# A decoder layer in float32: sums of squares on another engine, later forms, and form tiles at other offsets

## The chip, the cores and the metric

The kernel runs on one core of a Trainium2 chip, in one launch. The metric is the device time of that core in microseconds. Five engines run their own instruction streams: TensorE (matmuls), VectorE (DVE), ScalarE (ACT), GpSimd (POOL) and SyncE, which here issues DMAs. An engine takes its instructions in the order in which the program lists them, and one that waits holds all that stand behind it.

## The reference

One layer of a hybrid decoder: 512 tokens, width 2048, all float32. What matters here is its second half.

```python
mix = jnp.concatenate([ya, yb, yc], axis=-1)                 # three kinds of attention, normed
x = x + jnp.einsum('bse,ed->bsd', mix, w_out)
h = rmsnorm(x, ffn_norm)                                     # x / sqrt(mean(x*x)) * gain
u = causal_dwconv(jnp.einsum('bsd,df->bsf', h, w_up), conv_w, conv_b)    # width 3 along the tokens
gate, up = jnp.split(u, [D_FF], axis=-1)                     # D_FF = 5632
x = x + jnp.einsum('bsf,fd->bsd', jax.nn.silu(gate) * up, w_down)
```

## The kernel before

Activations lie with features on the partitions and the 512 tokens along the free axis, in 16 blocks of 128 features ("x block m", m = 0..15). Every float32 matrix is split into a high part, a cast to the matmul's format, and a low part, the rest. A product is three matmuls: high x high, low x high, high x low. Casts run on ACT, rests on DVE.

**Order.** The program is one long list that Python generators write: each task issues a few instructions and yields, and a clock in the kernel (lines 22 to 113) books every instruction on a model of its engine (for DVE 0.2 us + elements per partition/960, for GpSimd 0.2 + /480) and lets a task go on when the model says that its engine is there. What an engine executes is the order in which tasks came to write. Since every compute operation is recorded through one helper, all have line 51 in the profile; SyncE's DMAs have line 129, GpSimd's accumulating DMAs line 1044.

**Second half of the output projection.** Sixteen products (m = 0..15) of 24 matmuls of 128x512 accumulate into `pj`. After each runs the task `projected(m)`: DVE multiplies `pj` by a row scale into `tq` and adds the reloaded x block (`xn`), ACT writes it scaled by the norm's gain into `xb`, SyncE stores it (`xm_dram`) and reloads block m+3 (`reload_x`, a ring of 4 buffers named `xn`), and `sumsq` squares the block on ACT and adds the square to `gacc`, on GpSimd. A buffer of `xn` can be reloaded when its old block has been stored and squared.

**Forms.** The up-projection works on pairs of x blocks (j = 0..7) and on halves of 256 tokens, with seven products in place of eight: each pair gives seven "forms" of 256 columns, the halves and sums of them, written by `even_forms(j)` (forms 0 and 3, from block 2j) and `odd_forms(j)` (forms 5, 1, 2, 4, 6). High parts are in the tiles `th0` to `th7`, low parts in `tl0` to `tl7`, 7 x 256 columns each. Sums are made in tiles `sm`. In the program before all of these tiles start 128 bytes after a multiple of 512, and the weights' `hi` and `lo` tiles on a multiple of 512.

**Up-projection.** There are 44 units of 128 rows of w_up. Each has seven steps, with the weights a11, p, q, a12, v, r, a22 and the forms 0, 3, 5, 1, 4, 2, 6 in this order; p = block(1,0) + block(1,1), v = block(0,0) + block(1,0), q = p + a11, r is made of others on DVE. A step is 8 pairs x 3 matmuls of 128x256 into `s`: for k = 0..7 high weight x `th`k, high weight x `tl`k, low weight x `th`k. In the profile they are `s<-th,hi`, `s<-tl,hi`, `s<-th,lo`; in the steps 0 and 1 of unit 0 the weights lie in `wh` and `wl`, two halves of 512 columns. a11, a12 and a22 are loaded by one DMA of 512 KB; p and v by a DMA and an accumulating one that GpSimd issues when the first has landed (`fetch`). The raw weights lie in `ld` and `wr`, three buffers each in turn. For unit 0 q is one DVE add of 128x1024 (`first_sum`, `add_raw`), made during the output projection.

Step s of the up-projection waits, in the order of writing, until `ready` has "even" or "odd" of the pair k, and step 2 until the odd forms of pair 7. The norm's factor is needed from step 6.

Of the kernel before, what the change touches and what calls it, by code (L numbers as in the profile page):

```python
# [29 lines left out]
PAD = 152  # L30
# [88 lines left out]
def program(tc, xT, w_in, w_out, w_up, w_down, small, table, consts, onehot, lognum, out):  # L119
# [24 lines left out]
    with ExitStack() as ctx:  # L144
# [175 lines left out]

        def sumsq(pool, acc, t, first):
            if first:
                scalar.activation(acc, t, AF.Square)
                return
            sq = yield from take(pool, rows[0])
            scalar.activation(sq, t, AF.Square)
            yield
            gpsimd.tensor_add(acc, acc, sq)
            give(sq)
# [613 lines left out]
        tr = tctx.enter_context(tc.tile_pool(name="tr", bufs=1, side="right", reuse_waits="tile"))  # L943
        cv = tx.tile([128, SM_N - SM_CONV], F32, name="conv")
        TH = [tp.tile([128, 7 * HS], F32R, name=f"th{j}") for j in range(8)]
        TL = [tp.tile([128, 7 * HS], F32R, name=f"tl{j}") for j in range(8)]
        load(cv, small[:, SM_CONV:])
        xs2, xb, quarters = [], [], {}

# [9 lines left out]
        def even_forms(j):  # L959

            a = xb[2 * j]
            while j > 1 and ("odd", j - 2) not in ready:
                yield 0.1
            f = quarters[j] = tr.tile([128, 4 * HS], F32, name="sm", bufs=2)
            scalar.copy(TH[j][:, :HS], a[:, :HS])
            vector.tensor_sub(f[:, :HS], a[:, :HS], a[:, HS:])
            yield
            scalar.copy(TH[j][:, 3 * HS:4 * HS], f[:, :HS])
            low(j, a[:, :HS], 0, 1)
            yield  # L970
            low(j, f[:, :HS], 3, 4)
            ready["even", j] = True

        def odd_forms(j):
            while j not in quarters:
                yield 0.1
            a, b, f = xb[2 * j], xb[2 * j + 1], quarters[j]
            q = [f[:, i * HS:(i + 1) * HS] for i in range(4)]
            vector.scalar_tensor_tensor(q[2], b[:, HS:], -1.0, q[0], op0=ALU.mult, op1=ALU.subtract)
            yield  # L980
            scalar.copy(TH[j][:, 5 * HS:6 * HS], q[2])
            scalar.copy(TH[j][:, HS:3 * HS], b)
            vector.tensor_sub(q[1], b[:, HS:], a[:, HS:])
            vector.scalar_tensor_tensor(q[3], q[2], -1.0, b[:, :HS], op0=ALU.mult, op1=ALU.subtract)
            low(j, q[2], 5, 6)
            yield
            scalar.copy(TH[j][:, 4 * HS:5 * HS], q[1])
            scalar.copy(TH[j][:, 6 * HS:], q[3])
            low(j, b, 1, 3)
            yield  # L990
            low(j, q[1], 4, 5)
            low(j, q[3], 6, 7)
            ready["odd", j] = True

        def projected(m):
            def task(pt):
                t = xs2[m]
                sq = yield from take(tx, "tq")
# [4 lines left out]
                yield  # L1003
                while m > 2 and ("odd", (m - 3) // 2) not in ready:
                    yield 0.1
# [8 lines left out]
                yield from (odd_forms if m % 2 else even_forms)(m // 2)  # L1014
                yield from sumsq(tx, acc, t, m == 0)
                if m == KT - 1:
                    yield
                    yield from row_rstd(tx, acc, D, r2, nr2)
                    ready["r2"] = True
# [14 lines left out]
        def fetch(u, name):  # L1034
# [3 lines left out]
            if u == NFF:  # L1038
                return load(t, w_down[0][DOWN.index(name)])
            first, second = {"a11": ((0, 0), None), "a12": ((0, 1), None), "a22": ((1, 1), None),  # L1040
                             "p": ((1, 0), (1, 1)), "v": ((0, 0), (1, 0))}[name]
            arrival = load(t, w_up[u, first[0], first[1]])
            if second:
                nc.gpsimd.dma_start(t, w_up[u, second[0], second[1]], accum_op=ALU.add)
                arrival += 4
            return arrival

        def add_raw(u, name, a, b):
            if u < NFF:
                first = u == 0 and name == "q"  # L1050
                t = got[u, name] = place() if first else tr.tile([128, 1024], F32, name="sm", bufs=2)
                vector.tensor_add(t, got[u, a], got[u, b])
# [22 lines left out]
        def first_sum():  # L1075
            while len(raws) < len(stream):
                yield 0.1
            yield max(raws[len(stream) - 1][1] - clock.now(), 0.01)
            fetch(0, "a12")
            add_raw(0, "q", "p", "a11")  # L1080

# [6 lines left out]
        wq = ctx.enter_context(tc.tile_pool(name="wq", bufs=1, reuse_waits="tile"))  # L1088
        while (0, "q") not in got:
            idle()  # L1090
# [16 lines left out]
        def w(t, i):  # L1107
            return cv[:, 4 * t + i:4 * t + i + 1]

# [73 lines left out]
        for s in range(7 * NFF):  # L1183
# [6 lines left out]
            if j == 3 and u + 1 < NFF:  # L1190
                for name in ("v", "a22") if u else ("a12", "v", "a22"):
                    fetch(u + 1, name)
            while s == 2 and ("odd", 7) not in ready or s == 6 and "r2" not in ready:
                idle()
# [10 lines left out]
            for k in range(8):  # L1205
                while ("even" if form in (0, 3) else "odd", k) not in ready:
                    idle()
# [156 lines left out]
```

## Time and profile before

| | us |
|---|---|
| median of 3 runs (lowest, highest) | 2162.34 (2160.52, 2177.22) |
| profiled execution | 2163.5 |
| its span | 2161.7 |
| TensorE busy in it | 2142.2 (99%) |
| DVE busy | 1460.8 (68%) |
| ACT busy | 1151.2 (53%) |
| GpSimd busy | 180.3 (8%) |

The span runs from the first to the last instruction of the profile; the time of the execution has some 2 us around it. By the chain of waits in time order attention and the input projection take the first 660 us, the output projection's second half ends at 788, the up-projection runs to about 1690 and the down-projection to the end. In a timeline row the columns are start, length, engine, line, operation, written tile <- read tiles and shape, and in brackets how long the engine was idle before and who released it. "Granted clock" 1.00 is 2.4 GHz, 0.50 is 1.2 GHz.

### The profile page before, as it was taken

To read this page: it belongs to the slowest core of one execution; us is meant where nothing else is said; L and a number is where in the kernel's file an instruction comes from. 1 tells how busy PE (TensorE), PEld (TensorE's weight loads), DVE (VectorE), ACT (ScalarE), POOL (GpSimd) and SP (SyncE) were. 2 spreads that over 40 slices of the span, in tenths; PEclk is the share of its full clock that TensorE was granted. 3 is DMA by queue.
4 is the path that set the end of the run, shared out by engine and by line. 5 is a ranking of instruction groups with operands and counts; after the bars stand their busy time and mean duration, and the time that the engine had idled before them with its cause. 6 is when DMAs were issued, how large, how long until landed. Compare 5 with 4: busy or idle time off the path is not lost.

```text
span 2161.7 us, 34584 instructions
## 1 busy us (share of the span) xinstructions
PE 2142.2 (99%) x13236; PEld 1926.7 (89%) x13236; DVE 1460.8 (68%) x2252; ACT 1151.2 (53%) x2043; POOL 180.3 (8%) x241
## 2 busy tenths in 40 slices
PE   8999999999999989999999999999999999999999
PEld 6888888888888879999999999999999888888887
DVE  7677777767765788888888888888888543322222
ACT  6778677767764555555555555555555333222221
POOL 4000101010000121000000000000000000000000
PEclk9999999999999999999999999999999999999999
DMA  6322344334566667777777777777776543533332
GB/s 198 106 93 84 100 145 137 112 102 144 194 200 200 200 178 214 186 210 194 200 198 197 209 191 198 198 200 197 198 205 179 178 166 132 173 110 117 117 117 73
DMA packets 124013, 353.82 MB, mean 164 GB/s; under 512 B 14328, under 2 KB 17784, under 8 KB 123848
## 3 DMA queue, kind: packets, MB, share of 16 engines
q1 hardware_dynamic: 111176, 305.47, 42.1%
q0 software_dynamic: 12672, 46.14, 12.9%
q8 instruction: 104, 1.70, 0.3%
q14 instruction: 61, 0.50, 0.1%
HBM read 312.18 MB, written 32.57 MB: 159 GB/s over the span
## 4 chain that ended last, share of the span: by engine, by line
PE 97%; DMA 1%; DVE 1%; issue 0%; SPq 0%; ACT 0%; POOLq 0%; DVEq 0%; ACTq 0%
PE s L51 51%; PE pj L51 42%; PE po L51 3%; PE c L51 2%; DMA wr<-in_w_up_dram 1%; SPq L129 0%; DVE wl L51 0%; DMA st<-in_xT_dram 0%; DVE sm L51 0%; DMA cst<-in_consts_dram 0%; DMA wr<-in_w_in_dram 0%; ACT x L51 0%; DVE sq L51 0%; DVE lo L51 0%; ACT hi L51 0%
## 5 line engine op out<-in xcount | busy, mean ns | idle before, releaser
L51 PE MATMUL s<-th,hi 128*128 128x256 f32 x2448 | 690.2, 282 | 1.4 <-ACT th L51 1.0
L51 PE MATMUL s<-tl,hi 128*128 128x256 f32 x2448 | 689.6, 282 | 1.3 <-DVE tl L51 1.3
L51 PE MATMUL s<-th,lo 128*128 128x256 f32 x2448 | 689.5, 282 | 0.0
L51 DVE TENSOR_TENSOR wl<-wr,wh 128x512 fp32r<-128x512 f32 (+2 forms) x424 | 297.7, 707 | 328.2 <-ACT wh L51 326.0
L51 ACT CAST wh<-wr 128x512 fp32r<-128x512 f32 (+2 forms) x424 | 252.9, 599 | 460.4 <-PE pj L51 319.7
L51 PE MATMUL pj<-x,wh 128*128 128x512 f32 x1504 | 473.5, 396 | 0.0
L51 PEld LDWEIGHTS s<-th,hi 128*128 128x128 f32 x2448 | 461.6, 189 | 2.1 <-ACT th L51 1.2
L51 PEld LDWEIGHTS s<-tl,hi 128*128 128x128 f32 x2448 | 461.5, 189 | 1.7 <-DVE tl L51 1.5
L51 PEld LDWEIGHTS s<-th,lo 128*128 128x128 f32 x2448 | 461.5, 189 | 0.0
L51 PEld LDWEIGHTS pj<-x,wh 128*128 128x128 f32 x1504 | 271.4, 188 | 51.1 <-issue 3.0
L51 PE MATMUL pj<-x,wl 128*128 128x512 f32 x752 | 294.3, 391 | 0.0
L51 PE MATMUL pj<-g,wh 128*128 128x512 f32 x620 | 190.8, 389 | 0.0
L51 DVE TENSOR_TENSOR lo<-sm,hi 128x1024 fp32r<-128x1024 f32 x87 | 106.6, 1225 | 100.5 <-ACT hi L51 100.5
L51 PEld LDWEIGHTS pj<-x,wl 128*128 128x128 f32 x752 | 141.2, 188 | 31.1
L51 ACT CAST hi<-sm 128x1024 fp32r<-128x1024 f32 x87 | 91.2, 1049 | 139.7 <-DVE sm L51 139.7
L51 DVE TENSOR_TENSOR lo<-wr,hi 128x1024 fp32r<-128x1024 f32 x111 | 135.5, 1221 | 25.9 <-ACT hi L51 25.9
L51 DVE TENSOR_TENSOR lo<-ld,hi 128x1024 fp32r<-128x1024 f32 x111 | 135.7, 1222 | 24.3 <-ACT hi L51 24.3
L51 PEld LDWEIGHTS pj<-g,wh 128*128 128x128 f32 x620 | 116.4, 188 | 24.1
L51 ACT CAST hi<-wr 128x1024 fp32r<-128x1024 f32 x111 | 116.7, 1051 | 19.7 <-PE s L51 14.7
L51 ACT CAST hi<-ld 128x1024 fp32r<-128x1024 f32 x111 | 116.6, 1050 | 18.8 <-PE s L51 15.6
L51 PE MATMUL pj<-g,wl 128*128 128x512 f32 x310 | 120.6, 389 | 0.0
L51 DVE CUSTOM_DVE_ANT_0 sc<-s,strip 128x128 f32<-128x128 f32 (+3 forms) x96 | 43.6, 455 | 74.6 <-PE s L51 74.2
(289 smaller groups left out, 3004.5 us busy)
## 6 DMA issues: line engine op xcount, KB each, us to landing
ld<-in_w_up_dram SPq DMA_DIRECT2D x111, 512.0 KB, 4.9
wr<-in_w_up_dram SPq DMA_DIRECT2D x109, 512.0 KB, 4.7
wr<-in_w_in_dram SPq DMA_DIRECT2D x78, 512.0 KB, 3.5
wr<-in_w_down_dram SPq DMA_DIRECT2D x78, 512.0 KB, 3.5
ld<-in_w_up_dram POOLq DMA_DIRECT2D x44, 512.0 KB, 5.5
wr<-in_w_up_dram POOLq DMA_DIRECT2D x44, 512.0 KB, 5.6
wr<-in_w_out_dram SPq DMA_DIRECT2D x32, 512.0 KB, 4.0
g_dram<-wl SPq DMA_DIRECT2D x44, 256.0 KB, 3.2
```

Source lines behind the costliest of these rows:

```text
L51: res = issue(out, *args, **kwargs)
```

## The change

1. `sumsq` in `projected` adds the squares to `gacc` on DVE.
2. Forms have a ready flag each. Pair 7 stops after forms 5 and 1, pair 6 before the low parts of forms 4 and 6, until step 1 of the up-projection is being written ("late"). `xb` of block m waits for form 2 of the pair that it takes the buffer from. The norm's factor is written when all sixteen squares are.
3. Unit 0's q is no DVE add but a load of block (1,0) and two accumulating DMAs, of (1,1) and of (0,0); a12 is fetched ahead of it.
4. The convolution's constants come in two loads, 152 columns into the tile `pad` (which held nothing before), 200 into `conv`. The tiles `th0` to `th6` are 16 bytes longer (their pitch becomes 7200 bytes), and a tile of 32 bytes, `end`, follows the forms. By the addresses of the program the tiles `th`j now start at 32(j-1) bytes against a multiple of 512, from -32 to 192, and all `tl`j at 192; `hi` and `lo` stay.

```diff
-        def sumsq(pool, acc, t, first):
+        def sumsq(pool, acc, t, first, engine=gpsimd):
...
-            gpsimd.tensor_add(acc, acc, sq)
+            engine.tensor_add(acc, acc, sq)
...
-        cv = tx.tile([128, SM_N - SM_CONV], F32, name="conv")
-        TH = [tp.tile([128, 7 * HS], F32R, name=f"th{j}") for j in range(8)]
+        cv = tx.tile([128, SM_N - SM_CONV - PAD], F32, name="conv")
+        TH = [tp.tile([128, 7 * HS + (4 if j < 7 else 0)], F32R, name=f"th{j}") for j in range(8)]
         TL = [tp.tile([128, 7 * HS], F32R, name=f"tl{j}") for j in range(8)]
-        load(cv, small[:, SM_CONV:])
+        vector.memset(tp.tile([128, 8], F32, name="end"), 0.0)
+        load(pad, small[:, SM_CONV:SM_CONV + PAD])
+        load(cv, small[:, SM_CONV + PAD:])
...
             scalar.copy(TH[j][:, 5 * HS:6 * HS], q[2])
             scalar.copy(TH[j][:, HS:3 * HS], b)
+            low(j, q[2], 5, 6)
+            yield
+            low(j, b[:, :HS], 1, 2)
+            ready["form 5", j] = ready["form 1", j] = True
+            while j == 7 and "late" not in ready:
+                yield 0.1
             vector.tensor_sub(q[1], b[:, HS:], a[:, HS:])
             vector.scalar_tensor_tensor(q[3], q[2], -1.0, b[:, :HS], op0=ALU.mult, op1=ALU.subtract)
-            low(j, q[2], 5, 6)
             yield
             scalar.copy(TH[j][:, 4 * HS:5 * HS], q[1])
-            scalar.copy(TH[j][:, 6 * HS:], q[3])
-            low(j, b, 1, 3)
+            scalar.copy(TH[j][:, 6 * HS:7 * HS], q[3])
+            low(j, b[:, HS:], 2, 3)
+            ready["form 2", j] = True
+            while j == 6 and "late" not in ready:
+                yield 0.1
             yield
             low(j, q[1], 4, 5)
             low(j, q[3], 6, 7)
-            ready["odd", j] = True
+            ready["form 4", j] = ready["form 6", j] = ready["odd", j] = True
 
         def projected(m):
             def task(pt):
+                while len(xs2) <= m:
+                    yield 0.1
...
-                while m > 2 and ("odd", (m - 3) // 2) not in ready:
+                while m > 2 and ("form 2", (m - 3) // 2) not in ready:
                     yield 0.1
...
-                yield from sumsq(tx, acc, t, m == 0)
-                if m == KT - 1:
+                yield from sumsq(tx, acc, t, m == 0, vector)
+                squares.append(m)
+                if len(squares) == KT:
...
-                             "p": ((1, 0), (1, 1)), "v": ((0, 0), (1, 0))}[name]
+                             "p": ((1, 0), (1, 1)), "v": ((0, 0), (1, 0)), "q": ((1, 0), (1, 1))}[name]
...
+            if name == "q":
+                nc.gpsimd.dma_start(t, w_up[u, 0, 0], accum_op=ALU.add)
+                arrival += 4
...
         def first_sum():
...
-            yield max(raws[len(stream) - 1][1] - clock.now(), 0.01)
             fetch(0, "a12")
-            add_raw(0, "q", "p", "a11")
+            yield max(fetch(0, "q") - clock.now(), 0.01)
+            ready["q"] = True
...
-            while s == 2 and ("odd", 7) not in ready or s == 6 and "r2" not in ready:
+            if s == 1:
+                ready["late"] = True
+            while s == 2 and any(("odd", x) not in ready for x in range(8)) or s == 6 and "r2" not in ready:
                 idle()
...
-                while ("even" if form in (0, 3) else "odd", k) not in ready:
+                while (f"form {form}", k) not in ready:
```

The written order moves with it, at the transition from the output projection to the up-projection. First SyncE's queue there. Before, the reloads of the x blocks 13, 14 and 15 are `xn_8031`, `xn_8090` and `xn_8141`, and the `ld` are a11, p and a12:

```order
L129 DMA xn_8031<-xab_dram_76 128x512
L129 DMA ld_8063<-in_w_up_dram 128x1024
L129 DMA xm_dram_77<-xn_7919 128x512
L129 DMA xn_8090<-xab_dram_76 128x512
L129 DMA ld_8117<-in_w_up_dram 128x1024
L129 DMA xm_dram_77<-xn_7974 128x512
L129 DMA xn_8141<-xab_dram_76 128x512
L129 DMA xm_dram_77<-xn_8031 128x512
L129 DMA ld_8201<-in_w_up_dram 128x1024
```

In the changed program the reloads of blocks 13, 14 and 15 are `xn_8046`, `xn_8191` and `xn_8196`; the three `ld` are a11, p and a12, `wr_8110` is the first block of q, `wr_8246` that of v:

```order
L129 DMA xn_8046<-xab_dram_76 128x512
L129 DMA ld_8052<-in_w_up_dram 128x1024
L129 DMA ld_8102<-in_w_up_dram 128x1024
L129 DMA ld_8108<-in_w_up_dram 128x1024
L129 DMA wr_8110<-in_w_up_dram 128x1024
L129 DMA xm_dram_77<-xn_7917 128x512
L129 DMA xn_8191<-xab_dram_76 128x512
L129 DMA xm_dram_77<-xn_8041 128x512
L129 DMA xn_8196<-xab_dram_76 128x512
L129 DMA wr_8246<-in_w_up_dram 128x1024
```

The reload of block 14 moved from between a11 and p to behind q, and that of block 15 with it.

ACT's rows of the changed program from the last split of w_out (`wh_8140`) on; `xn_7890`, `xn_7815` and `xn_8041` are the x blocks 10, 9 and 12, `wh_8212` and `wh_8268` the two halves of p:

```order
L51 CAST wh_8140<-wr_7998 128x512
L51 ACTIVATE tq1_8157<-xn_7890 128x512
L51 CAST wh_8162<-ld_8052 128x512
L51 CAST wh_8179<-ld_8052 128x512
L51 CAST th4_7408<-sm_7930 128x256 x2
L51 ACTIVATE xb_8188<-xn_7917,sm_80 128x512
L51 ACTIVATE xb_8193<-xn_8041,sm_80 128x512
L51 CAST wh_8212<-ld_8102 128x512
L51 ACTIVATE tq2_8218<-xn_7815 128x512
...
L51 CAST hi_8258<-ld_8108 128x1024
L51 CAST hi_8265<-wr_8110 128x1024
L51 CAST wh_8268<-ld_8102 128x512
L51 ACTIVATE tq1_8292<-xn_8041 128x512
```

The squares of blocks 9 and 12 now stand behind the splits of p, and that of block 12 behind those of a12 and q as well. In the program before the squares of blocks 11 (`xn_7919`) and 12 (`xn_7974`) stood between the splits of a11's two halves:

```order
L51 CAST wh_8181<-ld_8063 128x512
L51 ACTIVATE tq2_8192<-xn_7919 128x512
L51 ACTIVATE xb_8195<-xn_8031,sm_80 128x512
L51 ACTIVATE tq0_8206<-xn_7974 128x512
L51 CAST wh_8215<-ld_8063 128x512
L51 CAST wh_8233<-ld_8117 128x512
```

DVE's rows of the changed program, from the add into x block 14 (`xn_8191`) to the low form 0 of pair 6 (`tl6`); `wl_8180` is the low part of a11's second half, `tq1_8157` and `tq2_8218` are squares, `xn_8196` is block 15:

```order
L51 TENSOR_TENSOR xn_8191<-tq0_8198,xn_8191 128x512
L51 TENSOR_TENSOR wl_8180<-ld_8052,wh_8179 128x512
L51 TENSOR_TENSOR gacc_86<-gacc_86,tq1_8157 128x512
L51 SCALAR_TENSOR_TENSOR sm_8079<-xb_8188,sm_8079 128x256
L51 TENSOR_TENSOR tl4_7416<-sm_7930,th4_7408 128x256 x2
L51 TENSOR_TENSOR sm_8223<-xb_8193 128x256
L51 TENSOR_TENSOR wl_8213<-ld_8102,wh_8212 128x512
L51 TENSOR_TENSOR tq0_8233<-pj0_8175,r1_83 128x512
L51 TENSOR_TENSOR xn_8196<-tq0_8233,xn_8196 128x512
L51 TENSOR_TENSOR tl5_7417<-sm_8079,th5_7409 128x256
L51 TENSOR_TENSOR gacc_86<-gacc_86,tq2_8218 128x512
L51 TENSOR_TENSOR tl6_7418<-xb_8193,th6_7410 128x256
```

The squares' adds are new on DVE, and the adds into blocks 14 and 15 stand ahead of the low parts that the first step of the up-projection reads. From the row after these to the low form 0 of pair 7 there are 16 more instructions.

## Rows read from the trace of the kernel before

**Rows 1.** The page's first part: busy time, share and instructions by engine.

```profile
PE 2142.2 (99%) x13236; PEld 1926.7 (89%) x13236; DVE 1460.8 (68%) x2252; ACT 1151.2 (53%) x2043; POOL 180.3 (8%) x241
```

**Rows 2.** Chain of waits in time order: start, length, engine, tile, count.

```profile
674.36 113.61 PE pj L51 x501
788.82 4.00 DMA wr<-in_w_up_dram
793.57 7.08 DMA wr<-in_w_up_dram
...
813.41 872.64 PE s L51 x7326
```

**Rows 3.** Timeline of TensorE, from the end of the output projection.

```profile
792.78 0.38 PE L51 MATMUL s<-th,wh 128*128 128x256 f32 x1 [2.26 <-ACT th L51]
796.51 0.58 PE L51 MATMUL s<-tl,wh 128*128 128x256 f32 x1 [3.34 <-DVE tl L51]
796.88 0.41 PE L51 MATMUL s<-th,wl 128*128 128x256 f32 x1
797.10 0.41 PE L51 MATMUL s<-th,wh 128*128 128x256 f32 x1
...
805.41 0.39 PE L51 MATMUL s<-th,hi 128*128 128x256 f32 x1 [1.04 <-ACT th L51]
807.05 0.39 PE L51 MATMUL s<-tl,hi 128*128 128x256 f32 x1 [1.25 <-DVE tl L51]
807.94 0.58 PE L51 MATMUL s<-th,hi 128*128 128x256 f32 x1 [0.40 <-ACT wl L51]
```

**Rows 4.** Busy us of PE, PEld, DVE, ACT, POOL; clock; DMA share; GB/s.

```profile
701.00:788.00 87.00, 87.00 (x386) 72.07 (x385) 73.18 (x125) 49.13 (x97) 18.98 (x13) 1.00 0.62 193
797.00:801.00 4.00, 4.00 (x21) 4.00 (x21) 0.46 (x2) 0.70 (x2) 0.00 (x0) 0.50 0.86 250
808.00:812.00 4.00, 4.00 (x21) 4.00 (x22) 2.88 (x3) 1.48 (x3) 1.07 (x1) 0.59 0.12 23
```

**Rows 5.** Timeline of DVE in the transition.

```profile
778.52 0.68 DVE L51 TENSOR_TENSOR tl<-xb,th 128x512 fp32r<-128x512 f32 x1
779.12 2.71 DVE L51 TENSOR_TENSOR wl<-wr,wh 128x512 fp32r<-128x512 f32 x1
...
785.55 1.22 DVE L51 TENSOR_TENSOR wr<-ld 128x1024 f32<-128x1024 f32 x1
...
792.35 0.42 DVE L51 TENSOR_TENSOR sm<-xb 128x256 f32<-128x256 f32 x1
```

**Rows 6.** Timeline of ACT in the transition.

```profile
776.88 0.62 ACT L51 CAST wh<-wr 128x512 fp32r<-128x512 f32 x1 [1.03 <-PE pj L51]
...
789.10 1.03 ACT L51 CAST hi<-ld 128x1024 fp32r<-128x1024 f32 x1
...
791.50 0.40 ACT L51 CAST th<-sm 128x256 fp32r<-128x256 f32 x1
...
794.12 0.62 ACT L51 ACTIVATE tq<-xn 128x512 f32<-128x512 f32 x1
```

**Rows 7.** Timeline of SyncE's queue: x block 13.

```profile
769.90 0.32 SPq L129 DMA_DIRECT2D xn<-xab_dram  x1
```

**Rows 8.** DMA issues: tiles, queue, count, KB each, median us to landing.

```profile
ld<-in_w_up_dram SPq DMA_DIRECT2D x111, 512.0 KB, 4.9
ld<-in_w_up_dram POOLq DMA_DIRECT2D x44, 512.0 KB, 5.5
xn<-xab_dram SPq DMA_DIRECT2D x16, 256.0 KB, 3.8
```

**Rows 9.** Groups of TensorE's instructions by form: busy us, mean ns.

```profile
L51 PE MATMUL s<-st,st 128*128 128x256 f32 x96 | 17.8, 282 | 0.0
L51 PE MATMUL s<-akv,st 128*128 128x256 f32 x64 | 13.0, 289 | 0.0
L51 PE MATMUL po<-pt,av 128*128 128x256 f32 x64 | 9.0, 283 | 0.0
```

More of the change, by code (lines that the diff above doesn't have):

```diff
@@ L943, in program @@
         tr = tctx.enter_context(tc.tile_pool(name="tr", bufs=1, side="right", reuse_waits="tile"))
-        cv = tx.tile([128, SM_N - SM_CONV], F32, name="conv")
-        TH = [tp.tile([128, 7 * HS], F32R, name=f"th{j}") for j in range(8)]
+        cv = tx.tile([128, SM_N - SM_CONV - PAD], F32, name="conv")
+        TH = [tp.tile([128, 7 * HS + (4 if j < 7 else 0)], F32R, name=f"th{j}") for j in range(8)]
         TL = [tp.tile([128, 7 * HS], F32R, name=f"tl{j}") for j in range(8)]
-        load(cv, small[:, SM_CONV:])
-        xs2, xb, quarters = [], [], {}
+        vector.memset(tp.tile([128, 8], F32, name="end"), 0.0)
+        load(pad, small[:, SM_CONV:SM_CONV + PAD])
+        load(cv, small[:, SM_CONV + PAD:])
+        xs2, xb, quarters, squares = [], [], {}, []
         def reload_x(m):
@@ L971, in even_forms @@
             low(j, f[:, :HS], 3, 4)
-            ready["even", j] = True
+            ready["form 0", j] = ready["form 3", j] = True
         def odd_forms(j):
@@ L1049, in add_raw @@
             if u < NFF:
-                first = u == 0 and name == "q"
-                t = got[u, name] = place() if first else tr.tile([128, 1024], F32, name="sm", bufs=2)
+                t = got[u, name] = tr.tile([128, 1024], F32, name="sm", bufs=2)
                 vector.tensor_add(t, got[u, a], got[u, b])
@@ L1088, in program @@
         wq = ctx.enter_context(tc.tile_pool(name="wq", bufs=1, reuse_waits="tile"))
-        while (0, "q") not in got:
+        while "q" not in ready:
             idle()
@@ L1107, in w @@
         def w(t, i):
-            return cv[:, 4 * t + i:4 * t + i + 1]
+            c = 4 * t + i
+            return pad[:, c:c + 1] if c < PAD else cv[:, c - PAD:c - PAD + 1]
         def taps(c, x, t):
```

## The prediction

> **What bounds the kernel now.** I read the chain of waits first, then TensorE's timeline in the one place where that chain leaves TensorE, then the other engines and the SyncE queue in that place. TensorE is busy for 99% of the span [rows 1], so an edit that takes work from DVE, GpSimd or ACT pays only where TensorE waits for it. The chain shows where that is [rows 2]: the second half of the output projection is one TensorE row that ends at 787.97, the steady up-projection begins at 813.41 and runs 7326 matmuls at 872.64/7326 = 0.119 us, and between the two stand transfers of the first w_up blocks. This transition is the place of the change. In it TensorE idles five times [rows 3]: 2.26 and 3.34 us in step 0 (8 k blocks of 3 matmuls; the waits are for k = 7, the high and the low part of form 0 of the last pair), 1.04 and 1.25 us at the same k of step 2, and 0.40 us: 8.3 us in all. After a stall the clock is granted at 1.2 GHz for some us: 4 us at 0.50 and 4 us at 0.59 [rows 4], which cost about 2.0 and 1.6 us. So the transition loses about 12 us, and that is all that the moved work could give back.
>
> **The squares on DVE.** Fifteen adds of 128x512 leave GpSimd for DVE, each as long as DVE's other 512-wide instructions, 0.68 us, 0.60 start to start [rows 5]: 9 us. DVE was busy 73.18 of the 87 us of the output projection [rows 4], and one of its 512-wide instructions there took 2.71 us at the time of a GpSimd add, where 0.68 is usual [rows 5]; such stretched instructions fall away. DVE's real load stays under 87 us, TensorE does not wait in this stage, cost nothing. If that cover went, it would be 9 us at most. What the adds do change is the written order: the generator books each add on its own model of DVE, the model gets late, and everything that follows from DVE is written later. The order listings show it: SyncE's reload of x block 14 stood ahead of p's load; now it stands behind a11, p, a12 and q, and block 15 behind it. By the addresses in the two programs blocks 14 and 15 take the buffers of blocks 9 and 12, where they took those of 10 and 11.
>
> **What this chains in the transition.** Five links, each with its rows.
> (a) The reload of block 13 needs the square of block 10, which ACT now does behind the last split of w_out; that split ends at 776.88 + 0.62 = 777.5 [rows 6]. So SyncE issues block 13 at about 778.1, a11 at 778.5 and p at 778.9; before, block 13 went out at 769.90 [rows 7].
> (b) p is a load plus an accumulating GpSimd transfer. For v of this trace that took from 788.82 to 793.57 + 7.08 = 800.65, or 11.8 us [rows 2]. So p is whole at 790.7.
> (c) On ACT the square of block 9 stands right behind p's first split. ACT stands until 790.7, splits (0.62), squares (0.62) [rows 6], ends at 791.9; only then may block 14 be reloaded, and it lands 3.8 us later [rows 8], at 795.8.
> (d) On DVE the add into block 14 is queued ahead of `wl_8180`, the low part of a11's second half, which TensorE needs at matmul 14 of step 0. DVE: 795.8 + 2 x 0.68, so 797.2. TensorE gets to matmul 14 at 788.0 + 14 x 0.119 = 789.7 and idles 7.5 us there.
> (e) Behind it DVE needs one 512-wide and four 256-wide instructions (0.68 + 4x0.42 less overlaps, 1.9) until ACT can copy the next form of pair 6, at 799.1; ACT then has that copy (0.40), the splits of a12 and q (1.03 each) and of p's second half (0.62) before it squares block 12 (0.62): 3.5 with the overlaps off, 802.6 [rows 6]. Block 15 lands 3.8 us later, 806.4; DVE's add, one low form, one square's add and the low form 0 of pair 6 (2x0.68 + 2x0.42) end at 808.6. TensorE, at matmul 19, idles 10.8 us. The low form 0 of pair 7 has 16 DVE instructions up to and with it, by the listing: 2 of 1024, 3 of 512, 11 of 256 columns, 2x1.22 + 3x0.68 + 11x0.42 = 9.1 us [rows 5], less 0.08 overlap each, 7.8: it is there at 816.4, and TensorE idles 7.4 us more at matmul 22.
> Step 0 thus loses 25.7 us where it lost 5.6. The half clock after it stays, about 2 us, with another 0.8 for the eight matmuls between the stalls. Steps 2 and 3 keep between nothing and all of their 2.7 us of waits and 1.6 us of half clock, since DVE is by then no later than TensorE. After: 28.5 to 32.8; before: 12. The transition costs **16 to 21 us more, 19 taken**. The bounds are wider, since ACT and DVE are walked by hand: if p's second transfer takes as long as in the steady stage (5.5 us [rows 8] instead of 7.08) it is 2 to 3 less, since three waits hang on it; if GpSimd's two transfers for q hold up a12's and q's splits it is 5 more. So 12 to 27.
>
> **The smaller edits.** Readiness per form, and pairs 6 and 7 stopping before their late forms, let step 0 and 1 go on without forms 2, 4 and 6; their worth is in the stalls just walked (the 16 instructions would be 20 otherwise). q no longer costs DVE 1.22 us [rows 5] but two more accumulating transfers of 512 KB; q is needed only in step 2, after 818, and is whole near 799 (779.6 + 4.9 + 2 x 7.1, [rows 2, 8]), no cost. v and a22 stand ahead of step 0 still; v is needed in step 4. The convolution constants in two loads are one SyncE issue more, 0.3 us, while TensorE has 87 us of matmuls ahead: nothing.
>
> **The offsets.** In the program before every form tile starts at a multiple of 128 bytes. After it the high tiles start at -32, 0, 32 ... 192 against a multiple of 512, the low ones all at 192. Of 7392 matmuls 2464 read a tile at an odd multiple of 32, 6160 one that is not at a multiple of 128. The nearest rows are the attention's 256-column matmuls [rows 9]: both operands on 128, 282 ns; moving operand at 96, weights on 128, 289; both at 96, 283. All durations, with the first of a group in them. From these I bound the cost: 0 to 7 ns on 2464, 0 to +17 us. Below, the steady spacing says how much could be gained: at 1.2 GHz the matmuls follow each other by 0.22 us (796.88 to 797.10 [rows 3]), and half of that is 0.11 where 0.119 is taken, so up to 10 ns on 7392, 70 us, if the offsets were what holds them. No row shows a matmul that is faster off 128. I take 0, by the row of 283, which is nearest to 282.
> The Trainium skill ("SBUF — State Buffer", SBUF specs) says that SBUF has 16-byte cachelines and that each crossing to a new line costs; steps of 32 bytes cross no line more than before, and by that rule the rate stays. The same notes ("TensorE: Matmul & The Clock Gate") give columns / 2.4 GHz + 2.5 ns for matmuls in a row, an estimate of 109 ns for 256 columns; the trace's 119 is above it, and by that page up to 72 us could be had. The measurement decides what stands now; which cause holds the other 10 ns no row shows.
>
> **Sum.** Transition +19, offsets 0, all else 0. The profiled execution took 2163.5 us (span 2161.7), 1.2 over the median of 2162.3; the sum is laid on the median: **2181 us**, 0.9% slower, with its own range 2174 to 2190. About 1% (21.6 us) is what a measurement of this kernel can tell from no change.
>
> **Rivals.**
> *The offsets slow TensorE.* The 289 of [rows 9] is real, 7 ns on every matmul whose tile stands at 32 mod 64, and the transition is as above: 2162.3 + 19 + 17 = 2198, slower. Against it: the median of those 64 would have to be high too, and the row's mean can be a few late ones. It decides from 1.1 ns on, where the sum passes 2184. Chance 0.22.
> *The offsets speed it up.* Some of the 10 ns comes from high, low and weight tiles standing alike. At 2 to 4 ns on 6160 matmuls it gives back 12 to 25 us: 2156 to 2169. From 7 ns on the kernel is over 1% faster (2138). For it: 0.119 is above half of the half-clock spacing. Against it: rows 9. Chance 0.2.
> *The reload chain does not bite.* If p is whole by 786, or ACT gets to the square of block 9 before p's split would hold it, blocks 14 and 15 come in time, TensorE waits only for DVE's order, and the late forms and the free GpSimd give back some 8 of the 12 us: 2154. Against it: the order puts the square behind the split, and a p loaded at 778.9 can't be whole in 7 us when its like took 11.8. Chance 0.13, with what else could shorten the chain.
>
> **How the numbers follow.** Forecast 0.45, the rivals 0.22, 0.2 and 0.13. Faster by over 1%: half of the second rival, and the third where it falls together with it, 0.13. Slower by over 1%: the first rival but for its mildest cases, 0.2, and the part of the forecast above 2184, a quarter, 0.13: 0.33. Within 1%: 0.54. Range: below it takes in the third rival and the milder second, to 2147; above the first rival with some of the transition's upper bound, to 2204. Outside are the strong gains and the two upper bounds together.
>
> **What would show it.** TensorE's timeline of the new kernel from 788 on: idle stretches at matmuls 14, 19 and 22 of step 0, of some 7.5, 10.8 and 7.4 us, ended by DVE's `wl` and `tl`; ACT standing before 791 for a w_up transfer, with the square behind it; reloads of x at about 792 and 802.6 on SyncE; no idle TensorE before 787.9. The steady chain: 0.119 us for each of 7300 matmuls says that the offsets do nothing; 0.121 or more, or 0.117 or less, names the rival. The forecast is wrong if x block 14 goes out before 788, or if the steady spacing moves by more than 1 ns.

## The result and the profile after

Over 13 runs each, the changed kernel takes 2179.62 us in the median (2174.26 to 2183.21), the kernel before 2161.27 (2159.60 to 2177.22). The ratio of the undisturbed runs is 1.0069, 95% interval 1.0051 to 1.0086: 11 to 19 us slower. The changed kernel's runs fall into two groups, six from 2174.26 to 2175.13 and seven from 2179.62 to 2183.21; the profiled execution, 2174.56 with a span of 2172.8, is of the first, and the offsets explain both groups (below).

Busy time by engine, to [rows 1], and the chain of waits in time order, to [rows 2]:

```profile
PE 2137.1 (98%) x13236; PEld 1922.5 (88%) x13236; DVE 1455.9 (67%) x2275; ACT 1150.1 (53%) x2043; POOL 159.9 (7%) x228
```

```profile
674.07 102.50 PE pj L51 x452
778.67 6.59 DMA ld<-in_w_up_dram
785.95 5.55 DMA ld<-in_w_up_dram
829.06 868.17 PE s L51 x7326
```

The chain now leaves TensorE at p's two transfers (`ld`), 11 us before the last product ends. The steady stretch, the same 7326 matmuls, begins 829.06 - 813.41 = 15.65 us later than before and is 872.64 - 868.17 = 4.47 us shorter. Together that is the 11.1 us by which the span grew.

TensorE's timeline in step 0, to [rows 3]:

```profile
789.04 0.28 PE L51 MATMUL s<-tl,wh 128*128 128x256 f32 x1
797.25 0.58 PE L51 MATMUL s<-th,wl 128*128 128x256 f32 x1 [7.93 <-DVE wl L51]
...
807.38 0.58 PE L51 MATMUL s<-tl,wh 128*128 128x256 f32 x1 [8.69 <-DVE tl L51]
...
813.56 0.58 PE L51 MATMUL s<-th,wh 128*128 128x256 f32 x1 [5.38 <-ACT th L51]
815.35 0.58 PE L51 MATMUL s<-tl,wh 128*128 128x256 f32 x1 [1.20 <-DVE tl L51]
```

These are matmuls 14, 19, 21 and 22: 23.2 us of waiting where [rows 3] has 5.6 in this step. Of the waits in step 2 none is left, and one of 0.27 us stands at step 3; one of 0.73 us is new, at the norm's matmul ahead of step 4. The stretches by busy time and clock, to [rows 4]:

```profile
701.00:788.00 87.00, 87.00 (x388) 72.19 (x387) 63.06 (x125) 43.32 (x86) 1.01 (x1) 1.00 0.56 181
802.00:806.00 4.00, 0.00 (x0) 0.00 (x0) 0.64 (x2) 0.65 (x2) 0.00 (x0) 0.50 0.47 172
815.00:820.00 5.00, 4.66 (x22) 4.66 (x23) 4.11 (x10) 3.25 (x7) 0.87 (x1) 0.50 0.50 147
```

TensorE did not wait during the output projection, and DVE was busy for 63 of its 87 us, less than the 73 before, although eight of the squares' adds run there. Before, eight of its instructions there took 1.51 to 2.71 us, each at the time of a GpSimd add, as the one at 779.12 in [rows 5] beside this row:

```profile
779.68 1.58 POOL L51 TENSOR_TENSOR gacc<-gacc,tq 128x512 f32<-128x512 f32 x1
```

In the changed kernel no instruction of DVE on a tile takes over 1 us in this stretch. After the stalls 22 matmuls ran in 5 us at 1.2 GHz. DVE, to [rows 5]:

```profile
795.90 0.69 DVE L51 TENSOR_TENSOR xn<-tq,xn 128x512 f32<-128x512 f32 x1 [11.32 <-DMA xn<-xab_dram]
796.51 0.68 DVE L51 TENSOR_TENSOR wl<-ld,wh 128x512 fp32r<-128x512 f32 x1
...
805.36 0.69 DVE L51 TENSOR_TENSOR xn<-tq,xn 128x512 f32<-128x512 f32 x1 [4.89 <-DMA xn<-xab_dram]
```

DVE stands 11.32 us for x block 14 and 4.89 us for block 15, and `wl`, which TensorE waits for at 797.25, is the next instruction after the first. ACT, to [rows 6], and SyncE's queue, to [rows 7]:

```profile
776.60 0.62 ACT L51 CAST wh<-wr 128x512 fp32r<-128x512 f32 x1 [1.79 <-PE pj L51]
...
791.59 0.62 ACT L51 CAST wh<-ld 128x512 fp32r<-128x512 f32 x1 [6.53 <-DMA ld<-in_w_up_dram]
792.12 0.62 ACT L51 ACTIVATE tq<-xn 128x512 f32<-128x512 f32 x1
...
802.02 0.63 ACT L51 ACTIVATE tq<-xn 128x512 f32<-128x512 f32 x1
```

```profile
777.78 0.32 SPq L129 DMA_DIRECT2D xn<-xab_dram  x1
778.14 1.38 SPq L129 DMA_DIRECT2D ld<-in_w_up_dram  x3
...
792.77 0.33 SPq L129 DMA_DIRECT2D xn<-xab_dram  x1
...
802.67 0.32 SPq L129 DMA_DIRECT2D xn<-xab_dram  x1
```

ACT stands for p until 791.59, squares block 9, and at 792.77 block 14 is reloaded. At 802.02 it squares block 12, and at 802.67 block 15 is reloaded.

### The profile page after: what moved, and what is told of

It is laid out like the page before. It is cut to its first block, busy times and chain, and to the rows that moved or that the text cites. A ratio compares the mean times of both kernels' runs of the same rounds, so it can differ in the third digit from the quotient of the medians.

```text
span 2172.8 us, 34587 instructions
## 1 busy us (share of the span) xinstructions
PE 2137.1 (98%) x13236; PEld 1922.5 (88%) x13236; DVE 1455.9 (67%) x2275; ACT 1150.1 (53%) x2043; POOL 159.9 (7%) x228
## 4 chain that ended last, share of the span: by engine, by line
PE 96%; DVE 1%; DMA 1%; ACT 0%; issue 0%; SPq 0%; DVEq 0%; POOLq 0%; ACTq 0%
PE s L51 50%; PE pj L51 41%; PE po L51 3%; PE c L51 2%; DMA ld<-in_w_up_dram 1%; DVE wl L51 0%; DMA xn<-xab_dram 0%; SPq L129 0%; DMA wr<-in_w_in_dram 0%; DVE tl L51 0%; DMA st<-in_xT_dram 0%; DVE lo L51 0%; DVE gacc L51 0%; ACT hi L51 0%; DVE sm L51 0%
## 5 line engine op out<-in xcount | busy, mean ns | idle before, releaser
L51 PE MATMUL s<-th,lo 128*128 128x256 f32 x2448 | 690.2, 282 | 0.0
L51 PE MATMUL s<-tl,hi 128*128 128x256 f32 x2448 | 687.1, 281 | 0.0
L51 PE MATMUL s<-th,hi 128*128 128x256 f32 x2448 | 686.6, 280 | 0.3 <-ACT wl L51 0.3
L51 DVE TENSOR_TENSOR wl<-wr,wh 128x512 fp32r<-128x512 f32 (+2 forms) x424 | 293.6, 697 | 329.0 <-ACT wh L51 327.5
L51 ACT CAST wh<-wr 128x512 fp32r<-128x512 f32 (+2 forms) x424 | 252.6, 598 | 467.9 <-PE pj L51 326.8
L51 PE MATMUL pj<-x,wh 128*128 128x512 f32 x1504 | 473.8, 396 | 0.0
L51 PEld LDWEIGHTS s<-th,hi 128*128 128x128 f32 x2448 | 465.7, 190 | 0.7 <-ACT wl L51 0.5
L51 PEld LDWEIGHTS s<-tl,hi 128*128 128x128 f32 x2448 | 460.2, 188 | 0.2 <-issue 0.2
L51 PEld LDWEIGHTS s<-th,lo 128*128 128x128 f32 x2448 | 459.5, 188 | 0.0
L51 PEld LDWEIGHTS pj<-x,wh 128*128 128x128 f32 x1504 | 271.7, 188 | 50.9 <-issue 3.0
L51 PE MATMUL pj<-x,wl 128*128 128x512 f32 x752 | 294.6, 392 | 0.0
L51 PE MATMUL pj<-g,wh 128*128 128x512 f32 x620 | 191.1, 389 | 0.0
L51 DVE TENSOR_TENSOR lo<-sm,hi 128x1024 fp32r<-128x1024 f32 x87 | 106.6, 1226 | 99.6 <-ACT hi L51 99.6
L51 PEld LDWEIGHTS pj<-x,wl 128*128 128x128 f32 x752 | 141.3, 188 | 30.9
L51 ACT CAST hi<-sm 128x1024 fp32r<-128x1024 f32 x87 | 91.2, 1048 | 138.6 <-DVE sm L51 138.6
L51 DVE TENSOR_TENSOR lo<-ld,hi 128x1024 fp32r<-128x1024 f32 x111 | 136.0, 1225 | 23.0 <-ACT hi L51 22.9
L51 DVE TENSOR_TENSOR lo<-wr,hi 128x1024 fp32r<-128x1024 f32 x111 | 135.6, 1221 | 20.6 <-ACT hi L51 20.6
L51 PEld LDWEIGHTS pj<-g,wh 128*128 128x128 f32 x620 | 116.5, 188 | 24.1
L51 ACT CAST hi<-ld 128x1024 fp32r<-128x1024 f32 x111 | 116.7, 1052 | 17.3 <-PE s L51 15.0
L51 ACT CAST hi<-wr 128x1024 fp32r<-128x1024 f32 x111 | 116.8, 1052 | 15.3 <-PE s L51 14.3
L51 PE MATMUL pj<-g,wl 128*128 128x512 f32 x310 | 120.7, 389 | 0.0
L51 DVE CUSTOM_DVE_ANT_0 sc<-s,strip 128x128 f32<-128x128 f32 (+3 forms) x96 | 43.6, 455 | 74.6 <-PE s L51 74.2
```

Of the source, the lines that this page charges most:

```text
L51: res = issue(out, *args, **kwargs)
```

## The experiments

All use the kernel before or the changed kernel as base. "Steady start" and "steady length" are start and length of the chain's row `PE s L51 x7326`, as in [rows 2]. Each kernel has one trace, and the start of the same order differs by 2 us between two of them: 813.41 before, where the second transfer of v took 7.08 us [rows 2], and 811.35 in offsets_only, where it took 5.68. Differences of that size are not told from chance here.

| kernel | base | median us | ratio to before (95%) | steady start | steady length |
|---|---|---|---|---|---|
| before | | 2161.27 | 1 | 813.41 | 872.64 |
| changed | | 2179.62 | 1.0069 (1.0051, 1.0086) | 829.06 | 868.17 |
| offsets_only | before | 2162.96 | 1.0001 (0.9992, 1.0011) | 811.35 | 874.22 |
| no_offsets | changed | 2178.79 | 1.0088 (1.0073, 1.0103) | 829.10 | 872.64 |
| unbooked | changed | 2171.80 | 1.0046 (1.0033, 1.0059) | 818.8 | 874.7 |
| p_plain | changed | 2181.07 (one) | | 829.52 | 874.22 |
| two_squares_less | changed | 2162.95 | 1.0015 (1.0001, 1.0028) | 816.74 | 868.17 |
| squares_q_plain | changed | 2157.54 | 0.9987 (0.9974, 0.9999) | 812.43 | 874.22 |
| gpsimd_squares | changed | 2175.17 | 1.0065 (1.0049, 1.0080) | 822.23 | 868.17 |
| v_later | before | 2159.68 | 0.9991 (0.9979, 1.0003) | 809.57 | 872.62 |
| weights64 | before | 2160.10 | 0.9995 (0.9987, 1.0004) | 810.23 | 866.57 |
| weights64_v | before | 2158.21 | 0.9985 (0.9976, 0.9994) | 809.70 | 866.30 |
| forms64_v | before | 2152.81 | 0.9961 (0.9948, 0.9975) | 808.09 | 866.13 |

(unbooked: its row counts 7359 matmuls from 814.88 in 878.66 us; 33 of them, at 0.119 us, are taken off.)

### The chain of reloads

**p_plain.** `if u or name != "p":` ahead of p's accumulating transfer; block (1,1) is left out of p in unit 0.

> The changed kernel, with p of unit 0 loaded by its first transfer alone; block (1,1) is left out of it, so unit 0's second product is not the reference's. Same order on every engine. Theory of the chain p, split on ACT, square of block 9, reload of block 14, add, wl: p is there at about 785 instead of 791, so the reload of block 14 goes out at 787 instead of 792.8, and the wait at matmul 14 falls from 7.9 us to 1 to 4 us. Block 12's square stands behind q's split, which waits for q's transfers (about 799), so the wait at matmul 19 grows by most of what the first gave back: the whole changes by 2 to 5 us only. Rival, the order on DVE alone: the wait at matmul 14 stays near 8 us.

```profile
791.90 0.39 PE L51 MATMUL s<-th,wl 128*128 128x256 f32 x1 [2.27 <-DVE wl L51]
...
807.85 0.58 PE L51 MATMUL s<-tl,wh 128*128 128x256 f32 x1 [15.02 <-DVE tl L51]
```

In TensorE's timeline the wait at matmul 14 falls from 7.93 to 2.27 us, with block 14 reloaded at 787.14; the wait at 19 takes it all back, 15.02 for 8.69, since block 15 still goes out at 802.82. Links (b) to (d) are shown, and that removing one link of a chain moves the wait on. The time gains nothing, less than the 2 to 5 us expected: the steady start is 0.5 us later.

**two_squares_less.** In `projected`:

```diff
+                if m in (9, 12):
+                    sq = yield from take(tx, "tq")
+                    book(scalar, 0.22 + S / 1200)
+                    yield
+                    book(vector, 0.2 + S / 960)
+                    give(sq)
+                else:
+                    yield from sumsq(tx, acc, t, m == 0, vector)
```

> The changed kernel without the squares of x blocks 9 and 12 and their adds (the mean of squares lacks these two blocks); their time is still booked, so the order of all else is the same. Nothing holds the reloads of blocks 14 and 15 but their store. Theory of the chain: block 14 goes out near 780.5 and 15 near 786; the wait at matmul 14 (8 us) goes, the one at 19 falls from 9 to 2 to 4 us (p's split is still late, 791). Then q's split, which stands ahead of the last pair's copy on ACT and has q only near 800, is late next: matmul 21 waits 9 to 12 us instead of 6. In all 8 to 12 us less than the changed kernel. Rival, DVE's load or order: matmul 19 and 22 still wait, the sum of step 0 stays over 20 us.

```profile
791.11 0.39 PE L51 MATMUL s<-tl,wh 128*128 128x256 f32 x1 [0.69 <-DVE tl L51]
801.32 0.58 PE L51 MATMUL s<-th,wh 128*128 128x256 f32 x1 [9.70 <-ACT th L51]
803.02 0.58 PE L51 MATMUL s<-tl,wh 128*128 128x256 f32 x1 [1.12 <-DVE tl L51]
```

The waits at matmuls 14 and 19, 16.6 us, become 0.69; block 14 goes out at 778.28. But more changed than the two squares. By the addresses in the programs the buffers of `xn` are dealt out anew: block 13 takes that of block 8, and no longer that of block 10. It goes out 7.6 us earlier, with a11, p, a12 and q behind it, and p's first split stands at 786.48, not at 791.59 (SyncE's queue, then ACT):

```profile
770.17 0.32 SPq L129 DMA_DIRECT2D xn<-xab_dram  x1
```

```profile
786.48 0.62 ACT L51 CAST wh<-ld 128x512 fp32r<-128x512 f32 x1 [1.42 <-DMA ld<-in_w_up_dram]
```

What comes next is the wait expected, matmul 21, 9.70 us for 5.38. The steady start is 829.06 - 816.74 = 12.3 us earlier, where 8 to 12 were expected: the share of the whole chain, links (a) to (e) of the prediction together. How much (a) has of it by itself was not tried. DVE's adds are still there, all but two.

**squares_q_plain.** The same, and q's two accumulating transfers left out.

> As the kernel without the two squares, and q of unit 0 is its first transfer alone (two blocks of it are left out). q is there by 787. Theory: the wait at matmul 21 falls by another 6 us (it now waits for DVE's and ACT's order alone), the transition loses 14 to 16 us more than none, as before the change; time within 4 us of before. Rival: q's transfers were hidden, the time stays as without the squares.

```profile
797.01 0.58 PE L51 MATMUL s<-th,wh 128*128 128x256 f32 x1 [5.68 <-ACT th L51]
798.72 0.58 PE L51 MATMUL s<-tl,wh 128*128 128x256 f32 x1 [1.13 <-DVE tl L51]
```

Another 4.3 us (816.74 to 812.43): the wait for q's split on ACT, which the chain had covered. The transition then ends between the two starts of the old order (811.35 and 813.41), so that no cost of the late forms and the other adds on DVE shows; whether the late forms gain by themselves was not tried.

**unbooked.** `(nc.vector if engine is vector else engine).tensor_add(acc, acc, sq)`: the same instruction, without the entry in the generator's model of DVE.

> The changed kernel, but the squares' adds on DVE are issued without being booked on the generator's model of DVE, so the written order is about that of before (x block 14 reloaded ahead of p). Theory of the written order: the waits at matmuls 14 and 19 of step 0 go, since x blocks 14 and 15 are reloaded before 785, and step 0 loses 4 to 6 us as before; later something else is late: q, whole only after three transfers, is split on ACT ahead of p's second half, and TensorE waits some 10 us in step 1, and the norm's matmul stands early in step 2 and waits for the last add. In all 5 to 12 us over before, under the changed kernel. Rival, DVE's real load: the adds cost DVE their 9 us wherever they are written, step 0 still loses 20 us and more.

```profile
792.30 0.39 PE L51 MATMUL s<-tl,wh 128*128 128x256 f32 x1 [1.58 <-DVE tl L51]
800.03 0.58 PE L51 MATMUL s<-th,wh 128*128 128x256 f32 x1 [5.80 <-ACT wh L51]
803.84 0.58 PE L51 MATMUL s<-th,wl 128*128 128x256 f32 x1 [3.01 <-DVE wl L51]
...
812.80 2.08 PE L51 MATMUL c<-gacc,cst 128*128 128x512 f32 x2 [3.41 <-DVE gacc L328]
```

The time is in the expected range, 10 us over before. Step 0 waits 1.58 us (4 to 6 were expected) with all fifteen adds on DVE, and the loss is in step 1, where p's split on ACT stands behind q's, and at the norm's matmul, which is written too early. So it is the order, and not DVE's load, that made step 0 late.

**gpsimd_squares.** `sumsq(tx, acc, t, m == 0)`: the adds on GpSimd again.

> The changed kernel with the squares' adds back on GpSimd, all else kept. The written order is then that of before up to the last products (block 14 reloaded ahead of p). Theory of the written order: x block 14 goes out near 775, TensorE's waits at matmuls 14 and 19 for blocks 14 and 15 go; what stays is q behind three transfers, which ACT's splits and so step 0 and 1 wait for: 8 to 16 us over before, some 2 to 8 under the changed kernel. Rival: the late forms and the readiness of forms cause the loss, and step 0 has the changed kernel's four stalls.

Block 14 goes out at 774.42, as expected, and the total is in the range. But matmul 14 still waits, 6.25 us, against the expectation. GpSimd's and DVE's timelines show why:

```profile
783.45 0.87 POOL L1057 DMA_DIRECT2D wr<-in_w_up_dram  x1 [1.60 <-DMA xm_dram<-xn]
789.85 0.86 POOL L1060 DMA_DIRECT2D wr<-in_w_up_dram  x1 [5.53 <-DMA wr<-in_w_up_dram]
790.41 2.93 POOL L51 TENSOR_TENSOR gacc<-gacc,tq 128x512 f32<-128x512 f32 x2
```

```profile
792.03 0.69 DVE L51 TENSOR_TENSOR tq<-pj,r 128x512 f32<-128x512 f32 x1 [10.54 <-POOL gacc L51]
```

q's second accumulating transfer waits in GpSimd's queue for the first, the adds stand behind it, their `tq` buffers stay taken, and DVE waits 10.54 us for one. Parts 1 and 3 of the change hang together: in this order, adds behind q's transfers hold DVE up.

### The offsets

**offsets_only** (the kernel before with the fourth part of the change alone) and **no_offsets** (the changed kernel without it).

> The kernel before with the fourth edit alone (constants in two loads, form tiles at steps of 32 bytes). Theory: the offsets change TensorE's steady spacing from 118.67 to 118.05 ns, as in the trace of the changed kernel, and nothing else; 0.62 ns on 7300 matmuls is 4.5 us less, about 2157, ratio to before 0.998; the transition loses the same as before (waits of 2.3, 3.3, 1.0, 1.3 us at the same matmuls). Rival: the smaller spacing came with the other edits (GpSimd free of adds), and the spacing here stays 118.67, ratio 1.000.

> The changed kernel without the fourth edit (form tiles on multiples of 128 bytes again). Theory: the transition stays as in the changed kernel, idle at matmuls 14, 19, 21 and 22 of step 0 of about 23 us in all, x block 14 reloaded at 792.8, and the steady spacing is 118.67 again: 16 us over before, some 4.5 over the changed kernel. Rival: the offsets take part in the transition, and its stalls change by more than 2 us.

The transition of the changed kernel is the same with and without the offsets (829.06 and 829.10), so they have no part in it. On the kernel before it starts 2.06 us earlier with them (811.35), one wait of 1.98 us being left of the three in steps 2 and 3, as v's transfer came sooner. But the steady length of offsets_only is 874.22, longer than before, where the changed kernel has 868.17. Over all profiles the kernels with the new placement show one of these two lengths and nothing between, with 118.06 or 118.89 ns from one matmul to the next (matmuls 480 to 7300); those with all form tiles on one address show 118.67 or 117.78. The chains of offsets_only and of no_offsets:

```profile
811.35 874.22 PE s L51 x7326
```

```profile
829.10 872.64 PE s L51 x7326
```

The start times in the traces show what the two rates are. In the kernel before the mean distance is 118.6 to 118.7 ns at every place among the 24 matmuls of a step. In the new placement it differs by place, and the pattern repeats step after step: in the lower rate 112 to 124 ns, alike within 0.6 ns in the three traces that have it, in the higher another one, 115 to 123 ns, alike within 0.01 ns in four. The runs agree: offsets_only has three from 2155.93 to 2158.08 and eight from 2161.72 to 2167.45, two_squares_less seven to 2163.31 and three from 2169.05, and the profiled execution lies in the lower group wherever the length is 868.17. The lengths stand 874.22 - 868.17 = 6.05 us apart, the means of the groups 6.5 us in the changed kernel and 6.9 in offsets_only. In the mean of its runs the placement gives nothing: 1.0001.

**spacing.** No layer: 240 matmuls at a time in the up-projection's sequence, 14 placements in turn, five rounds.

> The disputed spacing by itself: nothing of the layer is computed. 14 placements of the 16 form tiles (and of the weights), each in 5 runs of 240 matmuls of 128x256 in the up-projection's sequence (high x th, high x tl, low x th, k = 0..7), started after waits of different lengths. Theory: with all tiles on one address against 128 bytes the spacing is 118.67 ns at every start; with the changed kernel's placement (32 byte steps, low tiles at 192) a run locks into one of two rates, 118.05 or 118.89 ns, and which one depends on the start, not on the program. Rival: the rate belongs to the placement alone, each placement has one value (118.05 or 118.89 came from something else in the kernel).

The chain of its first round, with the length of each run; in this order: all forms at 128, the new placement, all at 0, at 64, at 96 (and, at the end, forms at 128 with weights at 32, with weights at 64):

```profile
54.94 28.76 PE s L161 x218
...
84.15 28.81 PE s L161 x240
...
113.46 29.06 PE s L161 x240
...
143.02 28.55 PE s L161 x240
...
172.07 29.08 PE s L161 x240
...
405.64 29.08 PE s L161 x240
...
435.22 27.48 PE s L161 x240
```

| forms (weights on a multiple of 512) | ns from start to start, last 144 of 240 matmuls, five rounds |
|---|---|
| all at 128 (as before) | 118.64 to 118.65 |
| high 32(j-1), low 192 (the change) | 118.89 to 118.90 |
| all at 0; high 0, low 256 | 120.00 |
| all at 64; high 64(j-1), low 192; high 128, low 192; high 32(j-1), low 128 | 117.76 to 117.78 |
| high 128j, low 192 | 118.31 |
| all at 32 | 116.69 four times, 117.79 once |
| all at 96 | 119.97 to 120.03 |
| all at 16 | 118.66 four times, 113.33 once |
| all at 128, weights at 32 | 120.02 to 120.03 |
| all at 128, weights at 64 | 113.33 to 113.34 |

So the spacing hangs on the addresses of both operands, over 113 to 120 ns, with nothing else at work; and two placements show a second rate in one round of five. Theory and rival are each half right: mostly one rate for a placement, but not always, and here the new placement had 118.89 in all rounds, with the pattern of distances of the higher rate. What chooses the rate in an execution stays open.

**weights64** and **weights64_v.** `vector.memset(wq.tile([128, 16], F32, name="step"), 0.0)` ahead of the weights' tiles.

> The kernel before, with a tile of 64 bytes put ahead of the up-projection's weights, so that hi and lo start 64 bytes after a multiple of 512 and the form tiles stay 128 after one. In the spacing kernel this placement (weights 64, moving 128) gave 113.33 ns at each of five starts, where weights 0, moving 128 gave 118.64. Theory, the spacing belongs to the addresses of moving operand and weights together: 113.3 ns from step 2 on, 5.3 ns on 7344 matmuls, 39 us less than before, 2122, if splits and loads keep up; the transition as before. Rival, in the full kernel the weights' casts and loads or the other engines hold TensorE: the spacing stays between 116 and 118.7, less than 20 us gained.

> The kernel before with both: weights 64 bytes after a multiple of 512, and the split of v written at step 2. If the two are independent, the 39 us of the placement and the 1 to 3 us of the split add: 2119 to 2121.

The theory fell: 117.78 ns and not 113.33, so the spacing kernel's best figure did not carry over. Why is not shown. The rival's number came about, its reason (splits, loads, other engines) was not tested; the two kernels also differ in addresses, the form tiles standing 2048 bytes apart in the small one and 7168 in this. weights64_v is 1.9 us under weights64, not 2119 to 2121. The steady length is 866.57, 6.1 us less, but the down-projection, whose tiles moved too, took 302.49 us for its 299.21 of before, by the row of its 1320 matmuls in the same chain:

```profile
1851.31 302.49 PE pj L51 x1320
```

**v_later.** In `after(s)`, on the kernel before:

```diff
-            cast(s + 3)
-            rest(s + 3)
+            if s == 2:
+                cast(4)
+                rest(4)
+            if s != 1:
+                cast(s + 3)
+                rest(s + 3)
```

> The kernel before, with one thing moved: the split of v (step 4's weight) is written at step 2 and not at step 1, so that ACT does not stand for v's transfer (before: idle 2.97 us until 800.68) ahead of the copies of the last pair's late forms. Theory from the trace of before: the waits of step 2 (1.04 and 1.25 us) and the 0.40 us at step 3 go, with part of the second stretch at half clock; v's split in step 4 then waits up to 1.3 us. 2 to 4 us less than before, ratio 0.998 to 0.999. Rival: the wait only moves to step 4, no difference.

The waits of step 2 are gone and the steady start is 3.8 us earlier, but one of 1.21 us at the norm's matmul is new, and over the runs the interval holds 1: too small to call alone. Some 2 us of the 3.8 may be the long transfer of v in the trace of before.

**forms64_v.** v_later, and `vector.memset(tp.tile([128, 16], F32, name="end"), 0.0)` behind the form tiles.

> The kernel before with the split of v written at step 2, and a tile of 64 bytes behind the forms, so that all form tiles start 64 and not 128 bytes after a multiple of 512 (weights on a multiple, as before; the down-projection's tiles stay). In the spacing kernel this placement had 117.77 ns at all five starts, where 128 had 118.64. Theory: 0.9 ns on 7296 matmuls is 6.5 us, with the split's 1 to 3 us some 2153, ratio 0.996. Rival, what the kernel with the weights at 64 showed: the spacing kernel's figure does not carry over to the full kernel, or locks into another rate; then 2158 to 2162.

```profile
808.09 866.13 PE s L51 x7326
...
1846.95 299.21 PE pj L51 x1320
```

Here the spacing kernel's figure did carry over (117.78 ns), the down-projection stays at 299.21, and all five runs lie between 2151.71 and 2153.10. It is faster than both kernels, 0.9961 of before; against v_later, which lacks only the placement, its steady length is 6.5 us less.

## Why the prediction was right, and where it was not

**The transition, +19 taken, 12 to 27.** Measured 15.65, by the steady starts. Link by link:

| | predicted | measured |
|---|---|---|
| (a) block 13, a11 issued | 778.1, 778.5 | 777.78, 778.14 |
| (b) p whole | 790.7 | 791.50 (785.95 + 5.55) |
| (c) block 14 issued, on DVE | 791.9, 795.8 | 792.77, 795.90 |
| (d) matmul 14, its wait | 797.2, 7.5 | 797.25, 7.93 |
| (e) block 15 issued, on DVE | 802.6, 806.4 | 802.67, 805.36 |
| (e) matmul 19, its wait | 808.6, 10.8 | 807.38, 8.69 |
| (e) matmul 22, the last wait | 816.4, 7.4 | 815.35, 5.38 + 1.20 |

The term that was most mis-sized is block 15's landing: 805.36 - 802.67 = 2.7 us, where the median 3.8 of [rows 8] was taken, a median over the whole program; the DMA share was 0.47 in 802:806, which may be why. Its 1.1 us, and some 0.9 us in which five matmuls ran at half clock ahead of matmul 19, which the prediction counts apart, make most of the difference of 2.5 us in step 0. Link (b) came near by luck, from two sizes that offset each other: p's first transfer took 6.59 us, not 4.00, and its second 5.55, not 7.08. Steps 2 and 3 kept almost none of their waits, at the low end of what was allowed. Leaving the two squares out, which freed block 13 too, shows that the chain (a) to (e) made 12.3 of the 15.65 us; the adds that were not booked show that the order alone set it off.

**The squares on DVE at nothing in the output projection.** Right: TensorE has no wait there.

**q's transfers at no cost.** Right in this kernel, but for a reason that was not given. q was not needed "only in step 2": its split stands ahead of the last pair's copy on ACT, which step 0 needs. The chain covered this; without the chain it costs 4.3 us (two_squares_less against squares_q_plain).

**The offsets at 0, between 0 and +17 us, or a gain.** The mean over runs is about 0, but the step failed as it was put: it asked what each matmul pays for its own tile's address, and took rows of single attention matmuls for it. No run shows such a price: in the new placement a matmul's distance goes by its place in the sequence, and the sequence runs at a rate that hangs on all addresses together. In the traces the new placement has two, 4.5 us under and 1.6 us over the old one. The Trainium skill ("SBUF — State Buffer", Specifications (TRN2)) would leave the rate as it was, since the steps cross no more 16-byte lines; the runs of the spacing kernel, 113.33 to 120.03 ns with every tile on a multiple of 16 bytes, do not agree with that.

**The rivals.** Neither rival on the offsets came about, nor the one without the chain. The thought behind the second, that time is lost by how high, low and weight tiles stand to each other, is borne out by the spacing kernel and by forms64_v; this placement did not collect it. The sum of terms, 2162.3 + 19, was 2181; what was measured on the base 2161.3 is 15.65 with -4.5 or +1.6: 2172.5 or 2178.5, and the groups' means are 2174.6 and 2181.1. The rest, 2.2 and 2.6 us, is most likely the trace of before, itself 2.2 us over the median of its kernel, with v's long transfer: from the start of offsets_only, 811.35, the transition is 17.7 us longer, and the sums are 2174.5 and 2180.6.

## What to carry to other kernels

When a generator with a model of the engines writes the order, the cost that an edit books moves everything that is written after it: read the new order of each queue around the edit and follow what stands behind a wait that was not there, as here a buffer that is reloaded only after a square behind a split behind a transfer. An experiment that takes something out of such a program can deal out the buffers anew: check what else moved. A ring of buffers whose release stands in another engine's queue is the place to look first. And two tiles' addresses are worth trying where TensorE is the bound: 64 bytes gained 6.5 us here, but measured in the kernel itself, since the small kernel's best placement did not carry over.

## What was not expected of the hardware

The distance between back-to-back 128x256 matmuls in this format hangs on the addresses of weights and moving operand: 113.33 to 120.03 ns in one kernel, at the same granted clock of 2.4 GHz. Some placements have two rates, 118.06 and 118.89 ns in the kernels with the new one. Each is a pattern of distances, 112 to 124 or 115 to 123 ns, that comes back with every 24 matmuls, and an execution keeps one of them over 7300 matmuls. So two groups of run times 6 us apart can come from a program's addresses.
